# Reordering the first loads, the second half's updates at phase borders, and the panels of one output projection

## The chip, the cores and the metric

The kernel runs on one core of a Trainium2 chip. The metric is the device time of one execution in microseconds (us). Three timed runs of the kernel before gave 2873.45, 2872.70 and 2874.04 us, a median of 2873.45 us. The change is judged against these.

## The reference

A residual stream h of 256 tokens by 2048 channels (fp32) goes through two layers of mixer and SwiGLU, and then through a second block:

```
for layer in range(2):
    u = rms_norm(h, mix_norm_pre[layer])
    if layer == 0: u = even_mixer(u, ...)   # stick-breaking attention (8 heads) + gated delta rule (8 heads)
    else:          u = odd_mixer(u, ...)    # block attention (8 heads) + dilated attention (8 heads)
    h = h + rms_norm(u, mix_norm_post[layer])
    u = swiglu(rms_norm(h, ffn_norm_pre[layer]), w_gate, w_up, w_down)
    h = h + rms_norm(u, ffn_norm_post[layer])
hn = rmsnorm(h, norm_gain); proj = hn @ w_in      # second block: pool mixer + state-space mixer
h = h + concat([ya, yb]) @ w_out
h = h + (p @ w_ple) * sigmoid(h @ w_ple_gate)
return rmsnorm(h, final_gain)
```

In the even mixer, `proj = u @ w_in` gives q, k and v of the attention heads and q, k, v and z of the delta heads; the heads' outputs side by side go through `mixed @ w_out`, the output projection. Nearly all of the arithmetic is in the dense products with fp32 weights.

## The kernel before

**Products.** The 256 tokens are two tiles of 128, t = 0 and t = 1. h lies in SBUF as [128, 2, 2048]. A dense product takes the contraction dimension in steps k of 128 channels (16 for 2048 channels) and the output columns in panels of 512. One k of one panel is a *unit*. Weights and activations are each split in a high part in fp32r and a rest, so a unit is three matmuls for each t (lines 313, 314, 315):

```
PE.matmul(o, a, wh, start=u["first"], stop=False)
PE.matmul(o, a, wl, start=False, stop=False)
PE.matmul(o, b, wh, start=False, stop=u["last"])
```

where a and b are the high part and the rest of the transposed activations (uh, ul), and wh and wl those of the weights. The results of a panel gather in one of four PSUM banks (`mm`); four more (`aux`) are for everything else.

**Weights.** SP loads them in chunks of two units, 512 KB (line 212, tile `wr`, five buffers). Each is then split: ScalarE (ACT) makes wh, with the gain of the norm as scale (line 347) or without (line 228), and VectorE (DVE) makes wl (line 348 or 229). `split(upto, most)` makes splits up to a look-ahead of three to six chunks, at most `most` of them at one step.

**Order.** The program is emitted by hand: each engine runs its instructions in the order in which the code issues them. `order()` (lines 238 to 275) lists the steps of all phases. A phase is a stretch of units behind one norm. Its first 12 units (`HEAD`) are done for t = 0 alone and then for t = 1 alone, the middle ones for both, and the last 8 (`TAIL`) again for t = 0 and then for t = 1. So, at a *border* between two phases, the norm of t = 0 can be worked off while the tail of t = 1 runs. Three kinds of *hooks* are tied to step numbers: T(t, c) transposes 512 channels of h on TensorE (line 364), which ACT and DVE then split to uh and ul (lines 344 and 345); U(t, c) adds a panel to the residual on DVE (line 425); C(t) makes the factor of the post norm. Four borders matter here: the two behind the mixers of the layers, and the two behind their FFNs. In the first phase there is no such border, and hooks there load x and make the first transposes.

**Tasks.** The work of the heads (attention, delta rule) runs in generators. After each unit `tick()` lets up to three of them take one step, each after the number of ticks that its last `yield` names. A generator can also wait for a flag, such as "v" in `T["ready"]`, which is set when the last unit of that panel has been issued. `drain(sel)` steps *all* tasks, over and over, until the ones in `sel` are done. In the even mixer, this happens eleven units into the output projection (line 1022), since its units from k = 12 on read the last heads' outputs.

**Start.** Line 137 loads the identity matrix for the transposes on ACT's queue; `run_units()` (line 277) starts x, the first weights and the gains' vector (`load_gains`, line 149; tile `gsrc`). The other gains are loaded by a task in the first phase, by SP, and transposed on TensorE at line 157.

Of the kernel before, what the change touches and what calls it, by code (L numbers as in the profile page):

```python
# [10 lines left out]
F32 = mybir.dt.float32  # L11
# [9 lines left out]
P = 128  # L21
# [76 lines left out]
def trunk(ctx: ExitStack, tc: tile.TileContext, I, out):  # L98
    nc = tc.nc
# [27 lines left out]
    def ct(name):  # L127
        a, b = _COLS[name]
        return cst[:, a:b]
# [4 lines left out]

    h = cp.tile([P, 2, D], F32, name="h")
    ident = cp.tile([P, P], F32, name="ident")
    nc.scalar.dma_start(ident, ct("ident"))

    def load_x(t, c, eng=nc.sync):
        eng.dma_start(h[:, t, c * 512:(c + 1) * 512], I["x"][0, t * P:(t + 1) * P, c * 512:(c + 1) * 512])  # L140
# [17 lines left out]
        ACT.activation(gT[:, first * KT:first * KT + n], ps[:, :n], AF.Copy)  # L158

    units, chunks, tasks, now = [], [], [], [0]  # L160
    phs = []

    def phase(norm=True, begin=None):
        phs.append(dict(a=len(units), norm=norm, begin=begin))

    def gemm(src, wap, kts, panels, evac, kc=2, gi=None):

        for j, (c0, c1) in enumerate(panels):
            n = c1 - c0
            for g in range(0, len(kts), kc):  # L170
                ks = kts[g:g + kc]
                chunks.append((wap, ks, c0, c1, gi))
                for i, k in enumerate(ks):
                    units.append(dict(chunk=len(chunks) - 1, i=i, k=k, src=src, n=n, j=j, ps={},
                                      first=g + i == 0, last=g + i == len(kts) - 1, evac=evac,
                                      before=[], after=[]))
                    units[-1]["pn"] = units[-1 - g - i]["ps"]

    def spawn(gen, gap=3, delay=1):
        tasks.append(Task(gen, gap, now[0] + delay))  # L180
# [1 line left out]

    def tick():
        now[0] += 1
        left = CAP
        for tk in list(tasks):
            if left and tk.next <= now[0] and tk.step(now[0]):
                left -= 1
                tasks.remove(tk)
                tasks.append(tk)  # L190
        tasks[:] = [tk for tk in tasks if not tk.done]

    def drain(sel):
# [44 lines left out]
    def order():  # L238

        seq = []  # L240
        ends = [p["a"] for p in phs[1:]] + [len(units)]
        for pi, (p, end) in enumerate(zip(phs, ends)):
            us = units[p["a"]:end]
            nx = phs[pi + 1] if pi + 1 < len(phs) else None
            nm = p["nm"] = p.get("nm") or Norm(p)
            head, mid, tail = us[:HEAD], us[HEAD:-TAIL], us[-TAIL:]
            T = lambda t, c, n=nm: (lambda: n.T(t, c))
            U = lambda t, c: (lambda: st["upd"](t, c))
            C = lambda t: (lambda: st["post"](t))
            hooks = {1: [T(0, 1)], 2: [C(1), U(0, 3)], 4: [T(0, 2)], 6: [U(1, 0), U(1, 1)],  # L250
                     HEAD - 2: [T(1, 0)], HEAD - 1: [T(1, 1)], HEAD - 4: [U(1, 2), U(1, 3)],
                     HEAD + 2: [T(1, 2)], HEAD + 4: [T(0, 3)], HEAD + 6: [T(1, 3)], HEAD + 5: [nm.stats],
                     HEAD + 10: []}
            if pi == 0:
                X = lambda c: (lambda: [load_x(t, c) for t in range(2)])
                hooks = {0: [nm.begin, T(0, 0), T(1, 0), X(2)], 2: [T(0, 1), X(3)], 3: [T(1, 1)],
                         6: [T(0, 2)], 7: [T(1, 2)], 9: [nm.stats], 10: [T(0, 3)], 11: [T(1, 3)],
                         HEAD + 3: [lambda: spawn(load_gains(1, len(gains)))]}
            if p["begin"]:
                hooks[HEAD + (10 if pi else 3)].append(p["begin"])  # L260
            if nm.norm:
                us[KT - 1]["before"].append(lambda n=nm: drain([n.task]))
            for i, (u, t) in enumerate([(u, 0) for u in head] + [(u, 1) for u in head]):
                if pi:
                    seq.append((u, (t,), hooks.get(i, []), EXTRA if t == 0 else 0, int(i > 1)))
            seq += [(u, (0, 1), hooks.get(i, []) if pi == 0 else [], 0, 99)
                    for i, u in enumerate(mid if pi else head + mid)]
            hooks = {}
            if nx:
                n2 = nx["nm"] = Norm(nx)  # L270
                hooks = {TAIL: [C(0)], TAIL + 3: [U(0, 0), U(0, 1)], TAIL + 5: [U(0, 2)],
                         2 * TAIL - 1: [n2.begin, lambda n2=n2: n2.T(0, 0)]}
            for i, (u, t) in enumerate([(u, 0) for u in tail] + [(u, 1) for u in tail]):
                seq.append((u, (t,), hooks.get(i, []), EXTRA if nx else 0, int(not nx or t == 0 or i == TAIL + 1)))
        return seq

    def run_units():
        load_x(0, 0)
        fetch(0)
        load_x(1, 0, nc.scalar)  # L280
        g0 = load_gains(0, 1)
        next(g0)
        fetch(1)
        for t in range(2):
            load_x(t, 1)
        fetch(3)
        logexp()
        for _ in g0:
            pass
        for u, ts, hooks, lead[0], most[0] in order():  # L290
            for f in hooks:
                f()
            if 0 in ts:
                for f in u["before"]:
                    f()
            fetch(max(u["chunk"] + LA, ns[0] + LA - 1))
            while (u["chunk"], u["i"]) not in W:
                split(ns[0])
            wh, wl, si = W[u["chunk"], u["i"]]
            if 1 in ts:  # L300
                del W[u["chunk"], u["i"]]
                live[si][0] -= 1
                if not live[si][0]:
                    del live[si]
            split(si + SA + lead[0], most[0])
            n = u["n"]
            xh, xl = u["src"](u["k"])
            for t in ts:
                if u["first"]:
                    u["ps"][t] = psm.tile([P, 512], F32, name="mm", tag="mm")  # L310
                o = u["pn"][t][:, :n]
                a, b = xh[:, t * P:(t + 1) * P], xl[:, t * P:(t + 1) * P]
                PE.matmul(o, a, wh, start=u["first"], stop=False)  # L313
                PE.matmul(o, a, wl, start=False, stop=False)  # L314
                PE.matmul(o, b, wh, start=False, stop=u["last"])  # L315
            if u["last"]:
                for t in ts:
                    u["evac"](u["j"], t, u["pn"][t][:, :n])
            if 1 in ts:
                for f in u["after"]:  # L320
                    f()
            tick()
# [197 lines left out]
    def mix1():  # L520
# [16 lines left out]
        def attn_head(g, T, mask, i, qT, kT):  # L537
# [22 lines left out]
            yield  # L560
            if "v" not in T["ready"]:
                yield lambda: "v" in T["ready"]
                yield 2
            mh, ml = st["m"]
            v = T["v"].rearrange("p t (h d) -> p t h d", h=4)
            po = aux()
# [11 lines left out]
        for g in range(4):  # L578
            T = dict(ready=set())
            base = (g // 2) * 3072 + (g % 2) * 512  # L580

            def start(g=g, T=T):
                for n in "qkv":
                    T[n] = t4("tm" + n).rearrange("p (t c) -> p t c", t=2)
                done.append(spawn(attn_group(g, T)))

            for i, n in enumerate("qkv"):
                b = len(units)
                gemm(u_src, win, KTS, [(base + 1024 * i, base + 1024 * i + 512)],
                     head_evac(lambda n=n, T=T: T[n], "rq" if n == "q" else "rs", "v"), gi=2)  # L590
                units[-1]["after"].append(lambda n=n, T=T: T["ready"].add(n))
                if i == 0:
                    units[b]["before"].append(start)
        c = len(units)
# [4 lines left out]
    def mix0():  # L599
# [97 lines left out]
        def gdn(g, T):  # L697
# [16 lines left out]
            ss = sp.tile([P, 4, 4], F32, name="gss", tag="gss", bufs=2)  # L714
            for ni, n in enumerate("qkv"):
                yield lambda: n in T["ready"]
                yield 2
                y = t4("c" + n).rearrange("p (h s) -> p h s", h=4)
                for hh in range(2):
                    ps = aux()  # L720
# [221 lines left out]
        def sb_head(g, T, i, qT, kT):  # L942
# [21 lines left out]
            T["s"] = True  # L964
            yield 1
            ACT.activation(zm, zm, AF.Exp)
            yield
            if "v" not in T["ready"]:
                yield lambda: "v" in T["ready"]
                yield 2  # L970
            mh, ml = st["mh"][0]
            v = T["v"].rearrange("p t (h d) -> p t h d", h=4)
            po = aux()
# [21 lines left out]
        for g in range(2):  # L995
            for kind, T, base in (("g", GT[g], 3072 + 512 * g), ("s", ST[g], 512 * g)):
                for i, n in enumerate("qkv"):
# [9 lines left out]
                    units[-1]["after"].append(lambda n=n, T=T: T["ready"].add(n))  # L1007
# [9 lines left out]
            gemm(u_src, win, KTS, [(6144 + 512 * g, 6656 + 512 * g)], z_evac(GT[g]), gi=0)  # L1017
            units[-1]["after"].append(lambda T=GT[g]: T["ready"].add("z"))
        c = len(units)
        gemm(h_src, I["ev_w_out"][0], KTS, cols(4), post_evac)  # L1020
        units[c]["before"] += [post_begin, lambda: load_post(I["mix_norm_post"][0])]
        units[c + 11]["before"].append(lambda: drain(list(done)))

    ssm = {}

# [585 lines left out]
```

## Time and profile before

| | |
|---|---|
| median of 3 runs | 2873.45 us |
| time of the profiled execution | 2871.88 us |
| span of its trace | 2870.1 us |
| mean granted TensorE clock | 0.994 of full speed |
| TensorE (PE) busy | 2819.5 us, 98% |
| VectorE (DVE) busy | 1771.5 us, 62% |
| ScalarE (ACT) busy | 1503.6 us, 52% |
| GpSimd (POOL) busy | 192.2 us, 7% |

The page of the profile gives each engine's busy time, with the matmuls and the loads of their weights (PEld) apart. Then come views of single stretches: a timeline lists instructions with start and length, and in brackets how long the engine stood idle before them and whom it waited for; a view of the waits sums that by what was waited for; a view of windows gives for a stretch the busy time of each engine and the clock that TensorE was granted (1.00 is 2.4 GHz, 0.50 is 1.2 GHz). The busy share of 98% is TensorE's, and it is an average: the 2% are not spread evenly.

### The profile page before, as it was taken

What the parts mean: (1) busy time and instruction counts of PE and PEld (TensorE: products, weight loads), DVE (VectorE), ACT (ScalarE), POOL (GpSimd) and SP (SyncE); (2) the same over time, 40 slices, a digit from 0 to 9 for tenths busy, and PEclk for the clock granted to TensorE, in tenths of its full rate; (3) what the DMA queues carried; (4) which work ended last, traced back from release to release, by engine and by line L of the source; (5) the groups of instructions that cost most, each with busy time, mean ns of one, the idle gap of its engine ahead of it and who ended that gap; (6) DMA issues with size and microseconds to landing.
All of it is one profiled execution on the core that took longest, in us unless ns stands there. A gap on an engine that the chain in (4) does not pass through costs nothing.

```text
span 2870.1 us, 36735 instructions
## 1 busy us (share of the span) xinstructions
PE 2819.5 (98%) x13503; PEld 2314.3 (81%) x13503; DVE 1771.5 (62%) x2701; ACT 1503.6 (52%) x2374; POOL 192.2 (7%) x290
## 2 busy tenths in 40 slices
PE   7999999999999999999999999999999999999998
PEld 5878877788888878878888878888888887878887
DVE  4776755678666666566666565545555556565555
ACT  4656554655555445446555465445544545555444
POOL 0140510000000011010000000000000001100000
PEclk9999999999999999999999999999999999999999
DMA  6564655576677767755556556666666665875654
GB/s 202 169 172 147 181 155 169 173 195 197 221 211 210 218 211 215 252 185 162 173 172 187 185 171 190 186 196 189 187 194 194 191 203 169 296 268 168 193 190 149
DMA packets 303621, 552.23 MB, mean 192 GB/s; under 512 B 43032, under 2 KB 48720, under 8 KB 303440
## 3 DMA queue, kind: packets, MB, share of 16 engines
q1 hardware_dynamic: 292896, 515.20, 58.9%
q0 software_dynamic: 10224, 34.35, 3.7%
q8 instruction: 106, 1.74, 0.2%
q14 instruction: 75, 0.61, 0.1%
q10 hardware_dynamic: 320, 0.34, 0.0%
HBM read 532.24 MB, written 21.76 MB: 193 GB/s over the span
## 4 chain that ended last, share of the span: by engine, by line
PE 94%; DVE 2%; ACT 1%; DMA 1%; issue 1%; SPq 0%; POOL 0%; ACTq 0%; POOLq 0%; DVEq 0%
PE mm L313 29%; PE mm L315 29%; PE mm L314 29%; PE aux L451 1%; DVE wl L348 1%; ACT wh L347 1%; PE aux L364 1%; PE aux L1344 0%; DMA wr<-in_ffn_w_up_dram 0%; DMA b<-in_b_im_dram 0%; DMA mb<-xs 0%; PE aux L1434 0%; PE aux L1203 0%; PE aux L540 0%; PE aux L567 0%
## 5 line engine op out<-in xcount | busy, mean ns | idle before, releaser
L348 DVE SCALAR_TENSOR_TENSOR wl<-wr,gT,wh 128x512 fp32r<-128x512 f32 x1248 | 881.8, 750 | 555.3 <-ACT wh L347 554.1
L347 ACT ACTIVATE wh<-wr,gT 128x512 fp32r<-128x512 f32 x1248 | 828.9, 716 | 529.9 <-PE mm L315 497.5
L313 PE MATMUL mm<-wh,uh 128*128 128x512 f32 x2624 | 1054.8, 402 | 1.3 <-ACT wh L347 1.3
L315 PE MATMUL mm<-wh,ul 128*128 128x512 f32 x2624 | 1028.1, 392 | 1.4 <-DVE ul L345 1.4
L314 PE MATMUL mm<-wl,uh 128*128 128x512 f32 x2624 | 1026.2, 391 | 0.2 <-DVE wl L348 0.2
L229 DVE TENSOR_TENSOR wl<-wr,wh 128x1024 fp32r<-128x1024 f32 x324 | 401.1, 1242 | 360.0 <-ACT wh L228 359.5
L315 PEld LDWEIGHTS mm<-wh,ul 128*128 128x128 f32 x2624 | 494.4, 188 | 110.9 <-DVE ul L345 5.3
L313 PEld LDWEIGHTS mm<-wh,uh 128*128 128x128 f32 x2624 | 495.3, 189 | 104.7 <-issue 5.7
L314 PEld LDWEIGHTS mm<-wl,uh 128*128 128x128 f32 x2624 | 495.5, 189 | 97.3 <-DVE wl L348 1.8
L228 ACT ACTIVATE wh<-wr 128x1024 fp32r<-128x1024 f32 x324 | 342.4, 1059 | 402.0 <-PE mm L315 397.2
L313 PE MATMUL mm<-wh,mh 128*128 128x512 f32 x832 | 326.5, 392 | 0.0
L315 PE MATMUL mm<-wh,ml 128*128 128x512 f32 x832 | 324.0, 389 | 0.0
L314 PE MATMUL mm<-wl,mh 128*128 128x512 f32 x832 | 323.8, 389 | 0.0
L313 PEld LDWEIGHTS mm<-wh,mh 128*128 128x128 f32 x832 | 156.2, 188 | 32.9 <-issue 1.4
L315 PEld LDWEIGHTS mm<-wh,ml 128*128 128x128 f32 x832 | 156.2, 188 | 32.7
L314 PEld LDWEIGHTS mm<-wl,mh 128*128 128x128 f32 x832 | 156.3, 188 | 31.5
L489 POOL TENSOR_TENSOR acc<-acc,wpost 128x512 f32<-128x512 f32 x12 | 15.3, 1300 | 789.7 <-ACT junk L335 789.7
L345 DVE TENSOR_TENSOR ul<-aux,uh 128x512 fp32r<-128x512 f32 x48 | 33.1, 689 | 56.0 <-ACT uh L344 55.8
L344 ACT ACTIVATE uh<-aux 128x512 fp32r<-128x512 f32 x48 | 28.5, 594 | 74.7 <-PE aux L364 74.7
L344 ACT ACTIVATE mh<-aux 128x512 fp32r<-128x512 f32 (+1 forms) x60 | 32.6, 543 | 52.5 <-PE aux L451 39.6
L345 DVE TENSOR_TENSOR ml<-aux,mh 128x512 fp32r<-128x512 f32 (+1 forms) x60 | 37.2, 619 | 36.3 <-ACT mh L344 35.3
L364 PE MATMUL aux<-ident,h 128*128 128x128 f32 x192 | 32.6, 299 | 8.8 <-DVE h L425 8.8
(445 smaller groups left out, 2014.1 us busy)
## 6 DMA issues: line engine op xcount, KB each, us to landing
wr<-in_ffn_w_gate_dram SPq DMA_DIRECT2D x176, 512.0 KB, 4.1
wr<-in_ffn_w_up_dram SPq DMA_DIRECT2D x176, 512.0 KB, 4.1
wr<-in_ffn_w_down_dram SPq DMA_DIRECT2D x176, 512.0 KB, 4.6
wr<-in_ev_w_in_dram SPq DMA_DIRECT2D x112, 512.0 KB, 3.8
wr<-in_od_w_in_dram SPq DMA_DIRECT2D x96, 512.0 KB, 3.7
wr<-in_w_in_dram SPq DMA_DIRECT2D x64, 512.0 KB, 4.9
wr<-in_ev_w_out_dram SPq DMA_DIRECT2D x32, 512.0 KB, 4.4
wr<-in_od_w_out_dram SPq DMA_DIRECT2D x32, 512.0 KB, 4.5
```

What stands on the lines that cost most here:

```text
L228: ACT.activation(hi, r[:, k:k + m, :], AF.Copy)
L229: DVE.tensor_sub(lo, r[:, k:k + m, :], hi.bitcast(F32))
L313: PE.matmul(o, a, wh, start=u["first"], stop=False)
L314: PE.matmul(o, a, wl, start=False, stop=False)
L315: PE.matmul(o, b, wh, start=False, stop=u["last"])
L344: ACT.activation(hi, src, AF.Copy)
L345: DVE.tensor_sub(lo, src, hi.bitcast(F32))
L347: ACT.activation(hi, src, AF.Copy, scale=gain)
L348: DVE.scalar_tensor_tensor(lo, src, gain, hi.bitcast(F32), OP.mult, OP.subtract)
L364: PE.transpose(p4[:, i * P:(i + 1) * P], h[:, t, k * P:(k + 1) * P], ident)
L451: PE.transpose(p4[:, i * P:(i + 1) * P], src[:, i * P:(i + 1) * P], ident)
L489: POOL.tensor_mul(acc, acc, cut(st["wpost"], j))
```

## The change

The changed kernel (a) loads the identity on SP's queue, and on ACT's queue the first gains ahead of x; (b) in the first phase does the first two units for t = 0 alone and then for t = 1, with the transposes T(1, 0) between them; (c) at borders moves U(1, 0) and U(1, 1) from step 6 to step 4 and U(1, 3) from step 8 to step 12, and makes at most one weight split at step 2 and at each step from 5 on (before: at each from 2 on), and one at the last tail step in place of one at the tail's second step for t = 1; (d) in the even mixer's output projection does k = 0 to 11 of panels 0 and 1 and then k = 12 to 15 of both, drains three tasks one after the other at units 0, 4 and 8, and all of them at unit 24; (e) sets the flags of q, k and v three ticks later, and drops the pause of two ticks that a task made after such a wait (some pauses stay), and one task waits 4 ticks instead of 2 behind an Exp. The weight vectors named in the diff's `load_gains` are loaded by the same lines as before.

```diff
-    nc.scalar.dma_start(ident, ct("ident"))
+    nc.sync.dma_start(ident, ct("ident"))
...
+        steps = [(j, 0, len(kts)) for j in range(len(panels))]
+        if late:
+            steps[:2] = [(0, 0, late), (1, 0, late), (0, late, len(kts)), (1, late, len(kts))]
...
     def tick():
         now[0] += 1
+        for d in [d for d in due if d[0] <= now[0]]:
+            due.remove(d)
+            d[1]()
...
+    def later(n, f):
+        due.append((now[0] + n, f))
...
     def drain(sel):
         while any(not x.done for x in sel):
+            for d in due:
+                d[1]()
+            due.clear()
...
-            hooks = {1: [T(0, 1)], 2: [C(1), U(0, 3)], 4: [T(0, 2)], 6: [U(1, 0), U(1, 1)],
-                     HEAD - 2: [T(1, 0)], HEAD - 1: [T(1, 1)], HEAD - 4: [U(1, 2), U(1, 3)],
-                     HEAD + 2: [T(1, 2)], HEAD + 4: [T(0, 3)], HEAD + 6: [T(1, 3)], HEAD + 5: [nm.stats],
+            hooks = {1: [T(0, 1)], 2: [C(1), U(0, 3)], 4: [T(0, 2), U(1, 0), U(1, 1)],
+                     HEAD - 2: [T(1, 0)], HEAD - 1: [T(1, 1)], HEAD - 4: [U(1, 2)],
+                     HEAD: [U(1, 3)], HEAD + 2: [T(1, 2)], HEAD + 4: [T(0, 3)], HEAD + 6: [T(1, 3)], HEAD + 5: [nm.stats],
...
-                hooks = {0: [nm.begin, T(0, 0), T(1, 0), X(2)], 2: [T(0, 1), X(3)], 3: [T(1, 1)],
+                hooks = {(0, 0): [nm.begin, T(0, 0), X(2)], (1, 0): [T(1, 0)], 2: [T(0, 1), X(3)], 3: [T(1, 1)],
...
-                    seq.append((u, (t,), hooks.get(i, []), EXTRA if t == 0 else 0, int(i > 1)))
+                    seq.append((u, (t,), hooks.get(i, []), EXTRA if t == 0 else 0, int(i == 2 or i > 4)))
+            if pi == 0:
+                seq += [(u, (t,), hooks.get((t, i), []), 0, 99) for t in range(2) for i, u in enumerate(head[:2])]
...
-                         2 * TAIL - 1: [n2.begin, lambda n2=n2: n2.T(0, 0)]}
+                         2 * TAIL - 1: [n2.begin, lambda n2=n2: n2.T(0, 0), lambda: split(len(parts), 1)]}
...
-                seq.append((u, (t,), hooks.get(i, []), EXTRA if nx else 0, int(not nx or t == 0 or i == TAIL + 1)))
+                seq.append((u, (t,), hooks.get(i, []), EXTRA if nx else 0, int(not nx or t == 0)))
...
     def run_units():
-        load_x(0, 0)
-        fetch(0)
-        load_x(1, 0, nc.scalar)
         g0 = load_gains(0, 1)
         next(g0)
+        load_x(0, 0)
+        load_x(1, 0, nc.scalar)
         fetch(1)
...
             for ni, n in enumerate("qkv"):
                 yield lambda: n in T["ready"]
-                yield 2
...
             ACT.activation(zm, zm, AF.Exp)
-            yield
+            yield 4
             if "v" not in T["ready"]:
                 yield lambda: "v" in T["ready"]
-                yield 2
...
-                    units[-1]["after"].append(lambda n=n, T=T: T["ready"].add(n))
+                    units[-1]["after"].append(lambda n=n, T=T: later(3, lambda: T["ready"].add(n)))
...
-        gemm(h_src, I["ev_w_out"][0], KTS, cols(4), post_evac)
+        gemm(h_src, I["ev_w_out"][0], KTS, cols(4), post_evac, late=12)
         units[c]["before"] += [post_begin, lambda: load_post(I["mix_norm_post"][0])]
-        units[c + 11]["before"].append(lambda: drain(list(done)))
+        for i, x in ((0, 2), (4, 4), (8, 1)):
+            units[c + i]["before"].append(lambda x=x: drain(done[x:x + 1]))
+        units[c + 24]["before"].append(lambda: drain(list(done)))
```

Three places show how instructions move. The first is ScalarE's program at its start, before: loads on its queue, the gains' copy (gT), the splits of x (uh) and of the weights (wh).

```order
L137 DMA ident<-in_cst_dram 128x128
L140 DMA h<-in_x_dram 128x512
L153 DMA gsrc<-in_mix_norm_pre_dram 16x128
L133 ACT_TABLE_LOAD
L158 ACTIVATE gT<-aux 128x16
L344 ACTIVATE uh<-aux 128x4x128 x2
L347 ACTIVATE wh<-wr,gT 128x512 x8
```

And after (the lines are numbered some 13 higher there):

```order
L153 DMA gsrc<-in_mix_norm_pre_dram 16x128
L140 DMA h<-in_x_dram 128x512
L133 ACT_TABLE_LOAD
L158 ACTIVATE gT<-aux 128x16
L358 ACTIVATE uh<-aux 128x4x128
L361 ACTIVATE wh<-wr,gT 128x512 x8
L358 ACTIVATE uh<-aux 128x4x128 x2
```

The second half's uh now stands behind eight wh. The second place is VectorE's program at the border from the first FFN to the odd mixer, before: residual updates (h), rests of the activations (ul) and of the weights (wl), the last tail result (acc) and the post norm's factor (ms).

```order
L425 SCALAR_TENSOR_TENSOR h<-acc,rp,h 128x512 x3
L345 TENSOR_TENSOR ul<-aux,uh 128x4x128
L485 TENSOR_TENSOR acc<-mm,acc 128x512
L345 TENSOR_TENSOR ul<-aux,uh 128x4x128
L329 TENSOR_REDUCE ms<-ssp 128x1
L330 TENSOR_SCALAR ms<-ms 128x1
L421 TENSOR_TENSOR acc<-acc,wpost 128x512
L425 SCALAR_TENSOR_TENSOR h<-acc,rp,h 128x512
L348 SCALAR_TENSOR_TENSOR wl<-wr,gT,wh 128x512 x4
L345 TENSOR_TENSOR ul<-aux,uh 128x4x128
L348 SCALAR_TENSOR_TENSOR wl<-wr,gT,wh 128x512 x4
L425 SCALAR_TENSOR_TENSOR h<-acc,rp,h 128x512 x4
```

And after, from the rest of the first transposes on:

```order
L359 TENSOR_TENSOR ul<-aux,uh 128x4x128
L362 SCALAR_TENSOR_TENSOR wl<-wr,gT,wh 128x512 x2
L499 TENSOR_TENSOR acc<-mm,acc 128x512
L359 TENSOR_TENSOR ul<-aux,uh 128x4x128
L343 TENSOR_REDUCE ms<-ssp 128x1
L344 TENSOR_SCALAR ms<-ms 128x1
L435 TENSOR_TENSOR acc<-acc,wpost 128x512
L439 SCALAR_TENSOR_TENSOR h<-acc,rp,h 128x512
L362 SCALAR_TENSOR_TENSOR wl<-wr,gT,wh 128x512 x2
L359 TENSOR_TENSOR ul<-aux,uh 128x4x128
L439 SCALAR_TENSOR_TENSOR h<-acc,rp,h 128x512 x2
L362 SCALAR_TENSOR_TENSOR wl<-wr,gT,wh 128x512 x4
```

Behind these stand one more h, two ul, the last h and three ul. The four updates of the second half, one piece before, now stand in three pieces, the first two ahead of four wl. The third place is VectorE's program where the last delta heads end in the even mixer's output projection, before: gf and gw are factors of the heads' norm, o the heads' outputs, mg their split parts.

```order
L843 TENSOR_REDUCE gf<-osq 128x4
L844 TENSOR_TENSOR gw<-grs 128x8
L845 TENSOR_TENSOR gf<-gf,gw 128x8
L846 TENSOR_SCALAR gf<-gf 128x8
L849 TENSOR_TENSOR gf<-gw,grs 128x8
L856 SCALAR_TENSOR_TENSOR o_3876<-o_3876,gf,tmz 128x128 x4
L856 SCALAR_TENSOR_TENSOR o_3910<-o_3910,gf,tmz 128x128 x4
L345 TENSOR_TENSOR mg<-aux,mg 128x4x128 x2
L229 TENSOR_TENSOR wl<-wr,wh 128x1024 x2
```

And after:

```order
L855 TENSOR_REDUCE gf<-osq 128x4
L856 TENSOR_TENSOR gw<-grs 128x8
L857 TENSOR_TENSOR gf<-gf,gw 128x8
L858 TENSOR_SCALAR gf<-gf 128x8
L242 TENSOR_TENSOR wl<-wr,wh 128x1024 x2
L861 TENSOR_TENSOR gf<-gw,grs 128x8
L242 TENSOR_TENSOR wl<-wr,wh 128x1024
L868 SCALAR_TENSOR_TENSOR o_3871<-o_3871,gf,tmz 128x128 x4
L868 SCALAR_TENSOR_TENSOR o_3910<-o_3910,gf,tmz 128x128 x4
L242 TENSOR_TENSOR wl<-wr,wh 128x1024 x2
L359 TENSOR_TENSOR mg<-aux,mg 128x4x128
L242 TENSOR_TENSOR wl<-wr,wh 128x1024
```

Before, the chain to mg has no weight split in it; after, five weight splits, two units each, stand between its members.

## Rows read from the trace of the kernel before

**Rows 1.** The page's head: span, and busy time of each engine.

```profile
span 2870.1 us, 36735 instructions
...
PE 2819.5 (98%) x13503; PEld 2314.3 (81%) x13503; DVE 1771.5 (62%) x2701; ACT 1503.6 (52%) x2374; POOL 192.2 (7%) x290
```

**Rows 2.** Waits of PE: what for, us in total, times, longest.

```profile
PE aux L157 <- DMA gsrc<-in_norm_gain_dram: 9.7, 1, 9.7
PE aux L364 <- DVE h L425: 8.8, 4, 2.2
PE aux L157 <- DMA gsrc<-in_mix_norm_pre_dram: 7.3, 1, 7.3
PE aux L451 <- DVE o L856: 4.5, 1, 4.5
PE aux L974 <- DVE tmv L1004: 2.6, 1, 2.6
PE aux L974 <- ACT zm L966: 1.6, 1, 1.6
```

**Rows 3.** Windows: length, busy us by engine (instructions), clock, DMA share, GB/s.

```profile
47.50:51.30 3.80, 3.73 (x10) 3.00 (x11) 1.64 (x4) 1.33 (x4) 0.00 (x0) 0.50 0.96 226
...
438.50:443.90 5.40, 5.18 (x16) 3.94 (x17) 3.39 (x10) 1.46 (x3) 0.00 (x0) 0.50 0.00 2
...
1283.61:1287.00 3.39, 2.82 (x11) 2.46 (x12) 3.01 (x5) 0.60 (x1) 0.00 (x0) 0.50 0.87 314
```

**Rows 4.** Timeline of the border behind the first FFN: start, us, engine, line.

```profile
1273.25 0.68 DVE L485 TENSOR_TENSOR acc<-mm,acc 128x512 f32<-128x512 f32 x1
...
1274.65 0.58 ACT L344 ACTIVATE uh<-aux 128x512 fp32r<-128x512 f32 x1
...
1277.39 2.73 DVE L348 SCALAR_TENSOR_TENSOR wl<-wr,gT,wh 128x512 fp32r<-128x512 f32 x4
...
1280.04 0.68 DVE L345 TENSOR_TENSOR ul<-aux,uh 128x512 fp32r<-128x512 f32 x1
...
1280.78 0.50 PE L315 MATMUL mm<-wh,ul 128*128 128x512 f32 x1 [0.69 <-DVE ul L345]
...
1281.11 0.40 PE L313 MATMUL mm<-wh,uh 128*128 128x512 f32 x1
...
1281.57 0.40 PE L315 MATMUL mm<-wh,ul 128*128 128x512 f32 x1
1283.29 2.73 DVE L425 SCALAR_TENSOR_TENSOR h<-acc,rp,h 128x512 f32<-128x512 f32 x4
...
1284.18 1.08 PE L364 MATMUL aux<-ident,h 128*128 128x128 f32 x4 [2.21 <-DVE h L425]
...
1289.21 0.60 PE L364 MATMUL aux<-ident,h 128*128 128x128 f32 x4
```

**Rows 5.** Timeline of the border behind the first mixer.

```profile
524.74 2.74 DVE L425 SCALAR_TENSOR_TENSOR h<-acc,rp,h 128x512 f32<-128x512 f32 x4
...
530.93 0.60 PE L364 MATMUL aux<-ident,h 128*128 128x128 f32 x4
```

**Rows 6.** Timeline of ACT in the even mixer.

```profile
364.30 2.02 ACT L886 ACTIVATE X<-mb 128x1024 f32<-128x1024 f32 x1 [7.28 <-DMA mb<-xs]
```

**Rows 7.** Timeline of the start.

```profile
9.99 5.00 ACT L347 ACTIVATE wh<-wr,gT 128x512 fp32r<-128x512 f32 x8
...
10.76 0.80 PE L313 MATMUL mm<-wh,uh 128*128 128x512 f32 x1 [1.30 <-ACT wh L347]
...
16.40 0.42 PE L364 MATMUL aux<-ident,h 128*128 128x128 f32 x1
```

**Rows 8.** DMA issues from 4.9 to 5.3 and 6.5 to 6.7 us: KB, us to landing.

```profile
wr<-in_ev_w_in_dram SPq DMA_DIRECT2D x1, 512.0 KB, 5.9
...
h<-in_x_dram SPq DMA_DIRECT2D x1, 256.0 KB, 6.3
```

**Rows 9.** Waits of SP from 33 to 41 us.

```profile
SPq L612 <- DVE cs L611: 6.2, 1, 6.2
```

More of the change, by code (lines that the diff above doesn't have):

```diff
@@ L160, in trunk, with gemm @@
     units, chunks, tasks, now = [], [], [], [0]
-    phs = []
+    phs, due = [], []
     def phase(norm=True, begin=None):
         phs.append(dict(a=len(units), norm=norm, begin=begin))
-    def gemm(src, wap, kts, panels, evac, kc=2, gi=None):
-        for j, (c0, c1) in enumerate(panels):
+    def gemm(src, wap, kts, panels, evac, kc=2, gi=None, late=None):
+        steps = [(j, 0, len(kts)) for j in range(len(panels))]
+        if late:
+            steps[:2] = [(0, 0, late), (1, 0, late), (0, late, len(kts)), (1, late, len(kts))]
+        pss = [{} for _ in panels]
+        for j, g0, g1 in steps:
+            c0, c1 = panels[j]
             n = c1 - c0
-            for g in range(0, len(kts), kc):
+            for g in range(g0, g1, kc):
                 ks = kts[g:g + kc]
@@ L173, in gemm @@
                 for i, k in enumerate(ks):
-                    units.append(dict(chunk=len(chunks) - 1, i=i, k=k, src=src, n=n, j=j, ps={},
+                    units.append(dict(chunk=len(chunks) - 1, i=i, k=k, src=src, n=n, j=j, pn=pss[j],
                                       first=g + i == 0, last=g + i == len(kts) - 1, evac=evac,
                                       before=[], after=[]))
-                    units[-1]["pn"] = units[-1 - g - i]["ps"]
     def spawn(gen, gap=3, delay=1):
@@ L264, in order @@
                 if pi:
-                    seq.append((u, (t,), hooks.get(i, []), EXTRA if t == 0 else 0, int(i > 1)))
+                    seq.append((u, (t,), hooks.get(i, []), EXTRA if t == 0 else 0, int(i == 2 or i > 4)))
+            if pi == 0:
+                seq += [(u, (t,), hooks.get((t, i), []), 0, 99) for t in range(2) for i, u in enumerate(head[:2])]
             seq += [(u, (0, 1), hooks.get(i, []) if pi == 0 else [], 0, 99)
-                    for i, u in enumerate(mid if pi else head + mid)]
+                    for i, u in enumerate(mid if pi else head + mid) if pi or i > 1]
             hooks = {}
@@ L309, in run_units @@
                 if u["first"]:
-                    u["ps"][t] = psm.tile([P, 512], F32, name="mm", tag="mm")
+                    u["pn"][t] = psm.tile([P, 512], F32, name="mm", tag="mm")
                 o = u["pn"][t][:, :n]
@@ L966, in sb_head @@
             ACT.activation(zm, zm, AF.Exp)
-            yield
+            yield 4
             if "v" not in T["ready"]:
                 yield lambda: "v" in T["ready"]
-                yield 2
             mh, ml = st["mh"][0]
@@ L1006, in mix0 @@
                     gemm(u_src, win, KTS, [(base + 1024 * i, base + 1024 * i + 512)], ev, gi=0)
-                    units[-1]["after"].append(lambda n=n, T=T: T["ready"].add(n))
+                    units[-1]["after"].append(lambda n=n, T=T: later(3, lambda: T["ready"].add(n)))
                     if i == 0:
```

## Prediction

> **What bounds the kernel now.** I read the page's head first: TensorE works 2819.5 of 2870.1 us [rows 1], so in most stretches nothing but its own matmuls sets the time, and an edit can only give back what lies in the other 50.6 us, or in stretches where it works at half clock. The second view is PE's waits [rows 2]. Six kinds make up most of the idle time: 9.7 and 7.3 us for the gains' vectors, 8.8 us in four pieces of up to 2.2 for the residual update h at phase borders, 4.5 us for the delta heads' outputs o, 2.6 us for an evacuated v (tmv), and 1.6 us for an Exp (zm). The third is the windows behind the waits [rows 3]: after three of these kinds of wait TensorE runs 3.4 to 5.4 us at a granted clock of 0.50, which is 1.2 GHz, though it has work. So a wait costs itself and about half of the stretch behind it. Then I read the timelines of these places to see who is late and why [rows 4 to 9].
>
> **Borders (part c).** At the border behind the first FFN, DVE makes four wl of 0.68 us each in one piece, twice, before it comes to the four updates of the second half at 1283.29; T(1, 0) waits 2.21 us for the first of them, and starts at 1284.18 [rows 4]. Before that, a product waits 0.69 us for ul. The window from 1283.61 on is 3.39 us at 0.50, which costs 1.7 [rows 3]. In all 2.21 + 0.69 + 1.7 = 4.6 us.
>
> The changed order on DVE, laid out with the durations of [rows 4] (0.68 for each of wl, ul, acc and an update): after the first ul two wl go first, from 1273.3 to 1274.65, so acc comes 1.4 us later than at 1273.25, and so does the square sum on ACT behind it and uh of T(0, 1), 1276.0 for 1274.65. Its ul ends at about 1277.3: TensorE's fifth unit waits 0.3. The factor, U(0, 3) and two wl follow to 1280.1; the ul of T(0, 2) ends at 1280.75, as before. Now come U(1, 0), U(1, 1), to 1282.1, four wl to 1284.75, U(1, 2), and the ul of T(1, 0), which ends at 1286.05. TensorE has T(1, 0)'s input at 1281.5 and starts it at 1281.75 without a wait; its eleventh unit waits 0.5 for the last wl needed; the first unit for t = 1 then waits 1.3 for that ul. With a matmul each 0.23 us (1281.11 to 1281.57 holds two steps [rows 4]), T(1, 2) comes at 1287.0 instead of 1289.21: 2.2 us gained. The same table for the border behind the second FFN gives 2.4. Behind a mixer there is no late acc, and U starts at 524.74 [rows 5]; laid out in the same way only a wait of 0.65 for ul stays, and T(1, 2) comes at 527.2 instead of 530.93: 3.7, twice. Sum: 2.2 + 2.4 + 7.4 = −12.0; I take −11.8, since the second mixer's row is a little shorter. What I choose here is that waits of at most 1.3 us leave the clock up. The row for it is the 0.69 us wait at 1280.78, behind which matmuls still follow at 0.23 [rows 4]; 2.21 us is followed by half clock. Between them no row tells, at full clock. The bounds: 0 if the waits and the clock stay as they are, and −18 if no wait is left (4.2 to 4.8 at each border).
>
> The Trainium skill, "TensorE: Matmul & The Clock Gate", section "What's actually happening", says that "the default state is throttled, and activity releases the throttle". By that, a wait shorter than the one removed could still bring the half clock; the rows agree that it follows waits of 2.2 us and more, and no row shows 1.3. By it the borders would give less, which is the second rival.
>
> **Output projection (part d).** Before, the drain eleven units in steps all tasks until the delta heads are done, so the chain gf, gw, o, mg is issued in one go with no unit between; TensorE waits 4.5 us for o [rows 2] and then runs 5.40 us at 0.50, 2.7 lost [rows 3]. After, all drains find their tasks done or near it, since thirteen units of 3 × 2 × 0.23 = 1.38 us, 17.9 us, are added ahead of the last one, and five weight splits stand between the members of the chain. What is next late is the last transposes of o, about one unit ahead of their use: at most 1.0 us is left. Four PSUM banks are held by panels 0 and 1; panel 2 starts four units (5.5 us) after panel 0 ends, which covers its evacuation. Term: −7.2 (range −7.2 to −6.2 with that, and +2 if the banks were late).
>
> **Even mixer (part e).** The 2.6 us wait for tmv is a product issued right behind the unit that ends v. With the flag three ticks later it comes at least two units, 2.8 us, behind: −2.6. The 1.6 us wait for zm goes too (4 ticks instead of 1 behind the Exp), but ACT stands 7.28 us for X at 364.30 [rows 6] and other small work of the heads is now queued behind it: I count 0 for the pair. Reordered tasks meet new places; no row shows how late each is. The nearest rows are the mixer's two waits of 1.6 and 2.6 us [rows 2]; I put +1.5, with −3 (the 1.6 and some others go) and +8 (three waits like 2.6) as ends.
>
> **Start (parts a, b).** The gains' vector heads ACT's queue and lands earlier, so the first product no longer waits for the second half's uh: about 7.9 instead of 10.76 [rows 7]. But only four unit halves follow; the rest needs uh of T(1, 0), which on ACT now stands behind eight wh of 0.63 us (5.00 for eight [rows 7]), and the last two of these need the fourth weight chunk. That chunk lands between those of 4.96 + 5.9 = 10.9 and 6.58 + 6.3 = 12.9 [rows 8], about 12.1. wh ends at 13.4, uh at 14.05, ul at 14.85, and T(0, 1) starts at 16.6 instead of 16.40: +0.2. So TensorE starts earlier and waits in the middle. Ends: −2.8 if the chunk comes early, +1.9 if the stretch after the new wait runs as the 3.80 us at 0.50 behind the 9.7 us wait did [rows 3], half of which is lost.
>
> **What stays.** The 9.7 us wait for norm_gain and its 1.9 of half clock: SP stands 6.2 us for a memset of DVE (cs) ahead of those loads [rows 9], and behind T(0, 1) all queues read as before. The splits made at other steps are hidden by DVE's 38% and ACT's 48% of idle time [rows 1], except at the borders, where they are in the table above.
>
> **Sum.** −11.8 − 7.2 − 2.6 + 1.5 + 0.2 = −19.9. The profiled execution took 2871.88 us (its span of 2870.1 and 1.8 around it), so 2852.0; the median of the runs is 1.57 higher, which gives **2853.5 us**. No change means within 0.2%, 5.7 us, about what a measurement can tell.
>
> **Rivals.**
> 1. *The wait moves to ul of T(1, 0).* At all four borders the wait of 1.3 comes out near the 2.2 that it replaces, and the clock still falls. For it: U(1, 2) and four wl stand ahead of that ul. Against: two updates are out of the way. Borders then give about −1: total −9, 2864. Chance 0.16.
> 2. *Short waits keep the half clock.* At each border the 1.7 stays, and 1.9 comes at the start: −19.9 + 6.8 + 1.9 = −11.2, 2862. For it: [rows 3] show it after each long wait; against: 1280.78 [rows 4]. Chance 0.10.
> 3. *No wait is left at all.* Borders −18, start −2.8, mixer −3, instead of my values: −19.9 − 6.2 − 3.0 − 4.5 = −33.6, 2840. For it: DVE has slack if ACT's square sum comes sooner than laid out. Chance 0.08.
> 4. *Slower: the dropped pauses make heads' products meet their evacuations.* Place: the eight attention heads' products with v and six convolution steps of the delta heads; each would wait as tmv does now, 2.62 us, 14 × 2.62 = 36.7. Without my +1.5 the rest is −21.4, so it decides from more than eight of the fourteen on; all would give +15.3, 2889. For it: the pause behind the wait is gone in both. Against: the flag is set three ticks later, which is as long as the pause and the tick it replaces. Chance 0.06.
>
> **Chances and range.** My forecast, with sizes off by a few us, 0.60. The range leaves the fourth rival out, and half of the third: 2844 to 2866. Faster by over 0.2% 0.87 (the forecast, the second and third, most of the first), same 0.07, slower 0.06.
>
> **What would show it.** Right: the line of waits for h gone or under 1 us, the wait for o gone, in the windows behind them a clock of 1.00, the wait for tmv gone, a new wait of TensorE around 10 to 14 us for uh of t = 1, and the wait of 9.7 unchanged. Wrong: windows at 0.50 behind waits for ul at the borders (rivals 1 and 2), or many new waits for tmq, tmk or tmv in the first 430 us (rival 4).

## The result, and the profile after

The changed kernel takes 2848.68 us (median of 4 runs, 2848.36 to 2849.59), the kernel before beside it 2873.74 (2872.70 to 2874.45): a ratio of 0.9914, with a 95% interval of 0.9896 to 0.9931. It is 25.1 us faster; 19.9 were forecast, and 2848.68 lies in the range of 2844 to 2866. The profiled executions took 2871.88 us before, 1.9 below that median, and 2849.59 after, 0.9 above its own, so the spans differ by only 22.3 us. The head of the page, after:

```profile
span 2847.8 us, 36740 instructions
...
PE 2811.0 (99%) x13503; PEld 2308.0 (81%) x13503; DVE 1771.2 (62%) x2701; ACT 1503.7 (53%) x2374; POOL 192.5 (7%) x290
```

Against [rows 1], TensorE has the same 13503 matmuls in 8.5 us less of busy time, which fits the half clock that went. The other 13.8 us of the span are idle time. PE's waits after:

```profile
PE aux L157 <- DMA gsrc<-in_norm_gain_dram: 10.6, 1, 10.6
PE mm L329 <- DVE ul L359: 3.5, 7, 0.9
PE aux L157 <- DMA ident<-in_cst_dram: 3.0, 1, 3.0
PE aux L378 <- DMA h<-in_x_dram: 2.9, 1, 2.9
PE mm L327 <- ACT uh L358: 2.4, 1, 2.4
PE mm L327 <- ACT wh L361: 1.3, 1, 1.3
PE aux L1357 <- DVE zs L1422: 0.7, 1, 0.7
```

Of the six lines of [rows 2] four are gone: h at the borders, o, tmv and zm. The 7.3 us for the first gains have become 3.0 for the identity and 2.9 for x, and the 9.7 us for norm_gain are 10.6. In place of h there are waits for ul, none over 0.9 us. The timeline of the border behind the first FFN, to be held against [rows 4] (the whole lies 16.1 us earlier now):

```profile
1263.98 0.68 DVE L359 TENSOR_TENSOR ul<-aux,uh 128x512 fp32r<-128x512 f32 x1
...
1264.59 1.41 DVE L439 SCALAR_TENSOR_TENSOR h<-acc,rp,h 128x512 f32<-128x512 f32 x2
...
1265.75 0.60 PE L378 MATMUL aux<-ident,h 128*128 128x128 f32 x4
...
1265.91 2.74 DVE L362 SCALAR_TENSOR_TENSOR wl<-wr,gT,wh 128x512 fp32r<-128x512 f32 x4
...
1269.22 1.28 DVE L359 TENSOR_TENSOR ul<-aux,uh 128x512 fp32r<-128x512 f32 x2
...
1269.96 0.50 PE L329 MATMUL mm<-wh,ul 128*128 128x512 f32 x1 [0.92 <-DVE ul L359]
...
1271.00 0.60 PE L378 MATMUL aux<-ident,h 128*128 128x128 f32 x4
```

The two updates now stand ahead of the four wl, and T(1, 0), at 1265.75, waits for nothing. The row at 1269.96 is the new wait, 0.92 us for the ul of T(1, 0). The border's first transpose is at 1271.35 before and at 1255.28 here; T(1, 2), at 1289.21 before and in the last row here, so comes 2.1 us sooner within the border. The waits there, 2.9 us before, are 1.3 now (0.40 and 0.92). The windows behind the places of [rows 3], after:

```profile
15.88:19.00 3.12, 3.12 (x9) 2.57 (x10) 0.00 (x0) 0.16 (x1) 0.00 (x0) 0.50 1.05 388
...
50.10:53.50 3.40, 3.40 (x9) 2.71 (x10) 1.90 (x4) 1.03 (x3) 0.00 (x0) 0.54 0.93 290
417.00:427.00 10.00, 10.00 (x54) 8.54 (x53) 4.69 (x7) 3.18 (x3) 1.04 (x1) 1.00 0.50 156
...
1268.00:1272.00 4.00, 3.08 (x16) 2.24 (x15) 3.17 (x5) 0.89 (x2) 0.00 (x0) 1.00 0.74 221
```

At the output projection (417 to 427) TensorE is busy throughout at full clock, and at the border the clock is full too. The start after:

```profile
8.54 0.80 PE L327 MATMUL mm<-wh,uh 128*128 128x512 f32 x1 [1.30 <-ACT wh L361]
...
11.69 2.70 ACT L361 ACTIVATE wh<-wr,gT 128x512 fp32r<-128x512 f32 x4 [1.36 <-DMA wr<-in_ev_w_in_dram]
...
14.29 0.57 ACT L358 ACTIVATE uh<-aux 128x512 fp32r<-128x512 f32 x1
14.92 0.50 PE L327 MATMUL mm<-wh,uh 128*128 128x512 f32 x1 [2.36 <-ACT uh L358]
...
17.75 1.05 PE L378 MATMUL aux<-ident,h 128*128 128x128 f32 x4
```

The first product comes 2.2 us earlier than in [rows 7], but the one at 14.92 waits 2.36 us for uh, which stands behind eight wh on ACT, and T(0, 1) is at 17.75 instead of 16.40.

The 0.50 from 15.88 on looks new, but the pace is not. In the kernel before, products stand 0.42 to 0.43 us apart from 12.14 up to T(0, 1), and 0.23 apart only from 17.50 on. Four products of before, two on either side of T(0, 1), and behind them its window view:

```profile
15.55 0.63 PE L314 MATMUL mm<-wl,uh 128*128 128x512 f32 x1
...
15.98 0.63 PE L315 MATMUL mm<-wh,ul 128*128 128x512 f32 x1
...
17.73 0.40 PE L315 MATMUL mm<-wh,ul 128*128 128x512 f32 x1
...
17.96 0.39 PE L313 MATMUL mm<-wh,uh 128*128 128x512 f32 x1
```

```profile
10.76:16.40 5.64, 5.64 (x12) 4.02 (x13) 5.37 (x9) 4.23 (x7) 0.00 (x0) 1.00 1.03 370
```

Two products of the changed kernel, inside the window at 0.50:

```profile
16.47 0.63 PE L327 MATMUL mm<-wh,uh 128*128 128x512 f32 x1
...
16.90 0.63 PE L328 MATMUL mm<-wl,uh 128*128 128x512 f32 x1
```

The steps are the same, 0.43 us, though one window says 1.00 and the other 0.50. So at the very start of a trace the steps of the products have to be read, and not that column.

From the starts of the same transposes in both traces, the time from the first transpose of abw (64.77 before, 66.96 after) on splits so, in us: the even mixer and its output projection to T(0, 0) of the first border 448.94, now 434.35 (−14.6); the four borders, first to last transpose of each, −3.6, −2.2, −3.5, −2.4 (−11.7 together); what lies before abw +2.2, of which 1.6 are there at T(1, 3) (33.00 for 31.38) and the rest comes with the longer wait for norm_gain; the rest of the trace, above all the second block, +1.8.

### The profile page after: what moved, and what is told of

Its sections match the earlier page's. It is cut to its first block, busy times and chain, and to the rows that moved or that the text cites. A ratio compares the mean times of both kernels' runs of the same rounds, so it can differ in the third digit from the quotient of the medians.

```text
span 2847.8 us, 36740 instructions
## 1 busy us (share of the span) xinstructions
PE 2811.0 (99%) x13503; PEld 2308.0 (81%) x13503; DVE 1771.2 (62%) x2701; ACT 1503.7 (53%) x2374; POOL 192.5 (7%) x290
## 4 chain that ended last, share of the span: by engine, by line
PE 94%; DVE 3%; DMA 2%; ACT 1%; issue 1%; SPq 1%; ACTq 0%; POOLq 0%; POOL 0%; DVEq 0%
PE mm L327 29%; PE mm L329 29%; PE mm L328 29%; DVE wl L362 1%; PE aux L465 1%; DMA wr<-in_w_in_dram 1%; PE aux L378 0%; ACT wh L361 0%; DVE h L439 0%; DVE ul L359 0%; PE aux L1357 0%; DMA wr<-in_ffn_w_up_dram 0%; DMA wr<-in_ev_w_in_dram 0%; DMA b<-in_b_im_dram 0%; PE aux L1447 0%
## 5 line engine op out<-in xcount | busy, mean ns | idle before, releaser
L328 PEld LDWEIGHTS mm<-wl,mh 128*128 128x128 f32 x832 | 156.3, 188 | 31.4
L358 ACT ACTIVATE mh<-aux 128x512 fp32r<-128x512 f32 (+1 forms) x60 | 32.4, 540 | 55.8 <-PE aux L465 39.6
L345 POOL TENSOR_TENSOR rp<-ms,half 128x1 f32<-128x1 f32 x8 | 6.7, 837 | 471.8 <-DVE ms L344 471.8
```

Of the source, the lines that this page charges most:

```text
L345: POOL.tensor_tensor(r[:, t:t + 1], m, half[:, 0:1], OP.pow)
L358: ACT.activation(hi, src, AF.Copy)
```

## The experiments

The first four do one part each on the kernel before. Their expectations were written with the two traces above at hand.

**Part (c) alone.**

```diff
-  4: [T(0, 2)], 6: [U(1, 0), U(1, 1)], HEAD - 4: [U(1, 2), U(1, 3)]
+  4: [T(0, 2), U(1, 0), U(1, 1)], HEAD - 4: [U(1, 2)], HEAD: [U(1, 3)]
...
-  int(i > 1)
+  int(i == 2 or i > 4)
```

> The kernel before with part (c) alone: the updates U(1, c) and the weight splits at borders. Theory: at each border the wait for h of 2.2 us goes, waits for ul of 0.4 to 1.1 us take its place, and the clock stays at 1.00; the four borders give 11.6 us, so about 2862, and start, mixer and output projection stay as they were (9.7, 2.6, 1.6 and 4.5 us of waits). Rival: the border gain needs the other parts (the tasks of part e stand on the same engines), and less than 8 us comes.

Measured: 2862.34 us, before 2873.43; ratio 0.9963 (0.9950 to 0.9977), 11.1 us. The wait for h is gone, and the waits for o, tmv and zm are as before; that for norm_gain is 10.8 for 9.7, and those for ul are 3.3 in six pieces for 1.4 in two. The interval alone (6.6 to 14.4 us) does not shut out the rival's 8, but the trace does: its four borders are 11.7 us shorter, as in the changed kernel. The theory holds.

**Part (d) alone.**

```diff
-  gemm(h_src, I["ev_w_out"][0], KTS, cols(4), post_evac)
+  gemm(h_src, I["ev_w_out"][0], KTS, cols(4), post_evac, late=12)
...
-  units[c + 11]["before"].append(lambda: drain(list(done)))
+  for i, x in ((0, 2), (4, 4), (8, 1)):
+      units[c + i]["before"].append(lambda x=x: drain(done[x:x + 1]))
+  units[c + 24]["before"].append(lambda: drain(list(done)))
```

(and `gemm` with the argument `late`, as in the change.)

> The kernel before with part (d) alone: panels 0 and 1 of the even mixer's output projection in two pieces, and the drains later. Theory: the wait of 4.5 us for o and 5.4 us at half clock go, 7.2 us, so about 2866.5. Rival: without the changed flags the last attention heads are still open at the earlier drains, which then step all tasks in one go and wait there, so that less than 4 us comes.

Measured: 2866.08 us; ratio 0.9975 (0.9966 to 0.9983), 7.4 us. No wait of PE shows from 420 to 450 us, and it works there without a gap at full clock:

```profile
427.00:433.00 6.00, 6.00 (x32) 5.10 (x31) 2.76 (x4) 2.12 (x2) 1.04 (x1) 1.00 0.59 173
433.00:440.00 7.00, 7.00 (x33) 5.79 (x32) 4.45 (x8) 2.88 (x3) 1.66 (x1) 1.00 0.47 154
```

The drains need nothing of part (e). The two edits of this part, the split panels and the later drains, were not run apart.

**Part (e) alone.**

```diff
-  units[-1]["after"].append(lambda n=n, T=T: T["ready"].add(n))
+  units[-1]["after"].append(lambda n=n, T=T: later(3, lambda: T["ready"].add(n)))
...
   ACT.activation(zm, zm, AF.Exp)
-  yield
+  yield 4
```

(and the pauses behind the waits dropped, as in the change.)

> The kernel before with part (e) alone: flags of q, k, v three ticks later, pauses dropped, 4 ticks behind the Exp. Theory: the waits for tmv (2.6 us), zm (1.6) and X (1.5) and some small ones in the mixer go, 7.4 us, so about 2866.3, with no change at the borders. Rival (the prediction's count): 1.1 us, as new waits take the place of some; then the other 6 us of the mixer came with the split of the output projection or by the shift in time that the start brings.

Measured: 2865.92 us; ratio 0.9973 (0.9963 to 0.9983), 7.5 us. From 80 to 500 us one wait of PE is left, the one that part (d) removes:

```profile
PE aux L460 <- DVE o L863: 4.5, 1, 4.5
```

The waits for tmv, zm and X are all gone, and no new one is there. The load of mb, from which X is made, is issued at 343.64 us here and at 356.96 before, and ACT no longer stands for it. The rival, the prediction's count of 1.1 us, is wrong. Which of the three edits of this part removes which wait was not run apart.

**Parts (a) and (b) alone.**

```diff
-  nc.scalar.dma_start(ident, ct("ident"))
+  nc.sync.dma_start(ident, ct("ident"))
...
-  hooks = {0: [nm.begin, T(0, 0), T(1, 0), X(2)], ...
+  hooks = {(0, 0): [nm.begin, T(0, 0), X(2)], (1, 0): [T(1, 0)], ...
...
```

(and the order of the loads in `run_units` and the steps of the first two units, as in the change.)

> The kernel before with parts (a) and (b) alone: loads of the start and first steps. Theory: the first product comes 2.2 us earlier, but TensorE then waits 2.4 us for uh of the second half and runs three us at half clock, so everything from 20 us on is 2.2 us later: about 2876. Rival (the prediction): +0.2, 2874; the rest of the 2.2 would be scatter between executions.

Measured: 2875.17 us; ratio 1.0007 (0.9998 to 1.0016). The interval takes in no change, so this run alone does not decide between the two. The four parts add up to −11.1 − 7.4 − 7.5 + 1.7 = −24.3, against −25.1 for all together.

The next ones start from the changed kernel. **Without (a) and (b).**

```diff
-  nc.sync.dma_start(ident, ct("ident"))
+  nc.scalar.dma_start(ident, ct("ident"))
...
-  hooks = {(0, 0): [nm.begin, T(0, 0), X(2)], (1, 0): [T(1, 0)], ...
+  hooks = {0: [nm.begin, T(0, 0), T(1, 0), X(2)], ...
...
```

(and the other lines of the two parts.)

> The changed kernel with parts (a) and (b) undone. Theory: the parts are additive, so it is faster than the changed kernel by what these two cost alone, 1.7 to 2.2 us: about 2846.7. Rival: the early stretch and the rest interact, and it comes out level with the changed kernel, 2848.7.

Measured: 2846.10 us (2845.72 to 2847.31); ratio to before 0.9905 (0.9890 to 0.9920). Its slowest run, 2847.31, is below the fastest of the changed kernel, 2848.36; the medians are 2.6 us apart. So the start costs time, as its traces show.

**Without (b) alone.**

```diff
-  hooks = {(0, 0): [nm.begin, T(0, 0), X(2)], (1, 0): [T(1, 0)], ...
+  hooks = {0: [nm.begin, T(0, 0), T(1, 0), X(2)], ...
...
```

(and the steps of the first two units as before.)

> The changed kernel with part (b) undone: the loads in the new order, but T(1, 0) ahead of the first product as before, so that uh of the second half stands before the weights' splits on ACT. Theory: the loss at the start is the order of uh behind eight wh, so the wait of 2.4 us and the half clock behind it go, and the first product comes at about 9.3 instead of 10.76: 3 us less than the changed kernel, about 2845.5. Rival: the fourth weight chunk (landing near 12) sets the pace in any case, and nothing is gained against the changed kernel.

Measured: 2845.27 us; ratio to before 0.9902 (0.9889 to 0.9916), 3.4 us less than the changed kernel.

```profile
9.23 0.79 PE L325 MATMUL mm<-wh,uh 128*128 128x512 f32 x1 [1.29 <-ACT wh L359]
...
14.00 0.60 PE L376 MATMUL aux<-ident,h 128*128 128x128 f32 x4
```

The first product is later than in the changed kernel (9.23 for 8.54), T(0, 1) is earlier (14.00 for 17.75), and no product in between waits for uh. So by the medians (b) costs 3.4 us and (a) gives 0.8, the latter within the scatter of the runs. The traces order the three starts without overlap: T(1, 3), the last transposes of this stretch, start at 29.8 to 31.4 us in the five kernels with the old start (before, at 31.38, is the latest of them), at 32.4 to 33.9 in the six with the new one, and at 28.55 here and 29.08 in the last run below, with the new loads and the old order.

**The other gains' loads first.**

```diff
+  def early():
+      g = load_gains(1, len(gains))
+      next(g)
+      spawn(g, delay=13)
...
-  HEAD + 3: [lambda: spawn(load_gains(1, len(gains)))]}
+  HEAD + 3: [early]}
```

> The changed kernel with one edit more: SP issues the five loads of the other gains ahead of the even mixer's constants instead of behind them; their transpose on TensorE stays where it is. Theory: the wait of 10.6 us is SP standing 6 us for DVE's memset of cs ahead of these loads; issued near 35 us they land near 40, so the wait falls under 1.5 us and the half clock behind it (about 1.9) goes: 11 us less, about 2837.5. Rival: another load behind them is late next (the weights that follow, or abw for the small projection), and less than 5 us comes.

Measured: 2842.69 us; ratio to before 0.9893 (0.9880 to 0.9907), 6.0 less than the changed kernel. The wait of 10.6 is gone, since the gains land before TensorE comes to their transpose. The rival's other load is there, but the gain is half of the theory's 11 rather than below 5:

```profile
PE aux L671 <- ACT abs L363: 4.5, 1, 4.5
```

```profile
49.60:52.40 2.80, 2.80 (x15) 1.89 (x15) 2.80 (x5) 1.89 (x4) 0.00 (x0) 0.52 0.65 249
```

The first row is of PE's waits, the second a window behind the wait: 4.5 us for abs, which is made from abw, and half clock.

**The old splits.**

```diff
-  int(i == 2 or i > 4)
+  int(i > 1)
...
-  2 * TAIL - 1: [n2.begin, lambda n2=n2: n2.T(0, 0), lambda: split(len(parts), 1)]}
+  2 * TAIL - 1: [n2.begin, lambda n2=n2: n2.T(0, 0)]}
```

(and the tail's second step for t = 1 makes a split again.)

> The changed kernel with the updates U where the change puts them, but the weight splits at borders as before (one at every step from 2 on, and one at the tail's second step for t = 1). Theory: the wait for h is removed by the place of U(1, 0) and U(1, 1) alone, ahead of four wl; the splits' places decide only which ul is late, so the borders keep about 10 of their 11.6 us: 2850. Rival: with a split at steps 3 and 4 four wl stay ahead of U(1, 0), the wait for h stays above 1.5 us and the clock falls: 2856 or more.

Measured: 2851.75 us; ratio to before 0.9925 (0.9912 to 0.9937). No wait for h is left; from first to last transpose the borders give 2.4, 2.2, 2.4 and 2.4 us. That is 9.4 of 11.7: the theory's 10, nearly. The splits' new places are worth 2.3 in the traces (3.1 by the medians), all of it behind the mixers.

**The old places of the updates, with the new splits.**

```diff
-  4: [T(0, 2), U(1, 0), U(1, 1)], HEAD - 4: [U(1, 2)], HEAD: [U(1, 3)]
+  4: [T(0, 2)], 6: [U(1, 0), U(1, 1)], HEAD - 4: [U(1, 2), U(1, 3)]
```

> The changed kernel with the updates U at their old steps (6 and 8), and the weight splits at borders where the change puts them. Theory: what decides is how many wl stand between the ul of T(0, 2) and the update U(1, 0); here two instead of four, so the wait for h falls from 2.2 to about 0.8 us, the clock stays at 1.00, and the borders keep some 9 of 11.6 us: 2851. Rival: the place of the updates alone removes the wait; here it stays near 2.2 with half clock behind it, and the time is 2858 or more.

Measured: 2851.89 us; ratio to before 0.9923 (0.9910 to 0.9937). Two rows of the timeline of the border behind the first FFN:

```profile
1265.42 1.40 DVE L362 SCALAR_TENSOR_TENSOR wl<-wr,gT,wh 128x512 fp32r<-128x512 f32 x2
...
1267.63 0.63 PE L378 MATMUL aux<-ident,h 128*128 128x128 f32 x4 [0.88 <-DVE h L439]
```

Two wl instead of four ahead of the update leave 0.88 of the 2.21 us, and the clock is not lost; the borders keep 9.0 us. Either half of part (c) does most of it by itself, because both shorten the same queue on DVE.

**Gains and abw first.**

```diff
+  st["abw"] = t2("abw", S).rearrange("p (k n) -> p k n", n=16)
+  nc.sync.dma_start(st["abw"], I["ev_w_in"][0][:, 7168:7184].rearrange("(k p) n -> p k n", p=P))
...
-  r = t2("abw", S).rearrange("p (k n) -> p k n", n=16)
-  nc.sync.dma_start(r, win[:, 7168:7184].rearrange("(k p) n -> p k n", p=P))
+  r = st["abw"]
```

(the new load stands in `early`, behind `next(g)`.)

> The changed kernel with the five loads of the gains and the load of abw (the small projection's weights) ahead of the even mixer's constants. Theory: with the gains alone ahead, 4.5 us of wait for abs and 1.9 us of half clock stayed, because abw was issued behind the same memset of cs and landed at 48; ahead of it, it lands near 42 and both go: about 2837. Rival: DVE's product with the gains stands behind ACT's copy gT and the memsets and is late by itself, or the next weight chunks now come later; then 2 us at most come, 2841.

Measured: 2840.44 us; ratio to before 0.9883 (0.9869 to 0.9896), 2.3 less than with the gains alone; at the first transposes of the first border it is 2.7 ahead (491.95 for 494.63). The rival's number is nearer: 1.8 us for abs stay. Two rows of the timeline ahead of it:

```profile
46.75 0.17 DVE L407 TENSOR_SCALAR rq<-rs 128x2 f32<-128x2 f32 x1 [2.94 <-POOL rs L405]
46.83 0.42 DVE L664 TENSOR_TENSOR abw<-abw,gT 128x256 f32<-128x256 f32 x1
```

DVE stands 2.94 us for the norm's factor from POOL, and the product with abw is queued behind that. The load is no longer what it waits for, and neither are the copy gT and the memsets that the rival named.

**The same, and (b) undone.**

```diff
-  hooks = {(0, 0): [nm.begin, T(0, 0), X(2)], (1, 0): [T(1, 0)], ...
+  hooks = {0: [nm.begin, T(0, 0), T(1, 0), X(2)], ...
```

> The kernel of the run before with part (b) undone as well, so that T(1, 0) stands ahead of the first product. Theory: the gains add up, 3.4 us for (b) undone and 11.5 for the loads: about 2834. Rival: the 3.4 us were partly time at which TensorE now waits for weights, since 385 to 390 GB/s are moved in the first 18 us in each of these kernels; then about 2836.

Measured: 2835.82 us (2834.06 to 2836.59); ratio to before 0.9867 (0.9854 to 0.9881). It is 12.9 us faster than the changed kernel, and the fastest of all here. The rival's 2836 is what came, but not for its reason: undoing (b) gave 4.6 us here, more than the theory's 3.4, and what is short are the loads, 8.2 for 11.5. In the traces T(1, 3) is 4.8 us ahead of the run before (29.08 for 33.85), and the first border 3.1 (488.85 for 491.95). The difference is half clock behind the wait for abs, which the run before does not have, with the same wait:

```profile
44.55:47.50 2.95, 2.95 (x15) 2.02 (x14) 2.80 (x5) 0.83 (x2) 0.00 (x0) 0.50 1.02 394
```

```profile
49.00:53.00 4.00, 4.00 (x38) 3.31 (x36) 3.12 (x5) 1.15 (x2) 0.00 (x0) 1.00 1.03 389
```

The first is of this kernel, behind a wait of 1.78 us, the second of the one before, behind 1.77. Why the clock fell in one of them only is not shown.

## Why the prediction was right, and where it was off

*Borders.* Right in mechanism and size: −11.8 forecast, −11.1 measured alone, −11.7 in the trace. The waits for ul came out at 0.9 us, under the 1.3 laid out, and the clock stayed up. That it would was a choice without a row; it is now shown for waits of up to 0.92 us here, and not for 1.3. Rivals 1 and 2 fall at the borders. Rival 3 falls there too (−11.1 for its −18) and at the start; only the mixer went its way, and beyond its −3.

*Output projection.* Right: −7.2 forecast, −7.4 measured alone. No wait is left there, so the four banks, two for each panel, were not late.

*Even mixer.* The term was mis-sized: −2.6 + 1.5 = −1.1 forecast, −7.5 measured, outside its own ends (−5.6 at the lower one). The step "I count 0 for the pair" fails: the wait for zm went, and X's went as well (1.5 us of PE, which the forecast had not priced), while the "+1.5" for new waits had nothing behind it in the run. What else went, some 1.8 us, is not accounted for. Part of it may be half clock behind tmv, which some executions have and others not (last section). The forecast also put the pause behind the Exp at one tick before; the heads' tasks step every two ticks, so it was 4 instead of 2, as the list of changes says. Rival 4 is refuted by the run of part (e): none of the fourteen products waits. Its counter-argument, that the flag's three ticks replace the pause, fits this; dropped pauses without the later flags were not run.

*Start.* The step "+0.2" was too low: 1.7 alone, 2.6 by undoing it, 1.6 in the trace at T(1, 3). The step that failed is "wh ends at 13.4". It let only the last two wh wait for a chunk of weights. In the run the last four stand until 11.69 for the third chunk, and end at 14.39. So uh ends at 14.86 (forecast 14.05) and ul at 15.83 (14.85), and T(0, 1) starts at 17.75 (16.6). The half clock behind the wait of 2.36 us is not what was missed: before has the same steps up to T(0, 1), and the forecast's own 2.55 us for the six products behind uh are 0.42 each. It does last longer: steps of 0.23 begin at 17.5 us before and at 19.3 in the changed kernel. The reference was late as well: with the old start T(0, 1) is at 16.40 in before and at 15.2 to 15.8 in the four other traces.

*What stays.* The wait for norm_gain stayed, and SP's 6.2 us for cs with it. It is 0.9 longer, because the load landed 5.1 us after its issue instead of 4.2. Nothing in its chain was changed, and of the ten traces that have this wait two show 9.7 and eight 10.5 to 10.9, among them three with the old start and one part alone. So it is scatter.

*Not forecast.* The rest of the trace is 1.8 us longer after, with 0.7 and 0.4 us of waits for zs and vw in the second block. The code of the second block is the same in all runs. From the last transposes of the fourth border to the first ones behind the second block, the thirteen traces take 334.5 to 337.1 us (before 334.5, after 336.1, part (c) alone 334.5), so it is scatter between executions; what makes it is not shown.

So the total is −19.9 − 6.4 (mixer) + 1.5 (start) + 0.7 (borders) − 0.2 (output projection) = −24.3, the sum of the four single runs; the error is the mixer's term, and the start hid a part of it. The two misses have opposite signs, but the range did not need that: without the start's 1.5 us it would still hold the time. One reading of the forecast goes too far: the half clock does not follow every wait "of 2.2 us and more", as the last section shows.

## What to carry to other kernels

Where TensorE is 98% busy, look for the few stretches where a short queue on another engine stands ahead of what it needs, and count the instructions between: here four wl of 0.68 us ahead of an update cost 2.2 us of waiting and mostly 1.7 of half clock at each border, and moving either the updates or the splits removes most of it. Starting the first product earlier gains nothing if the operand of the second half is then issued behind eight others on the same engine. When a wait is removed, read which load stands behind the same obstacle: behind the gains stood abw; moving the gains' loads alone gave 6.0 us, and both together 8.2.

## What the runs showed of the hardware that was not expected

In these traces the length of a wait does not decide whether the clock falls. The wait of 2.62 us for tmv is followed by full clock in before (first row below) and by half clock in the trace of part (c) alone (second row), though it is 2.62 us there too. And the same border wait of 2.21 us in one execution, that of part (d) alone, is followed by half clock behind the first FFN and by full clock behind the second mixer (the last two rows):

```profile
185.50:189.00 3.50, 3.50 (x16) 2.73 (x17) 3.28 (x6) 2.40 (x5) 0.00 (x0) 1.00 0.52 150
```

```profile
185.80:189.00 3.20, 2.89 (x8) 2.45 (x9) 2.48 (x6) 1.24 (x3) 0.00 (x0) 0.50 0.57 165
```

```profile
1278.00:1280.00 2.00, 2.00 (x8) 1.61 (x8) 2.00 (x4) 0.60 (x1) 0.00 (x0) 0.50 0.91 318
1669.50:1672.50 3.00, 2.27 (x14) 2.02 (x15) 3.00 (x5) 1.06 (x2) 0.00 (x0) 1.00 0.89 311
```

Four traces have the old borders, with 16 such waits of 2.2 us in all; behind 15 of them the clock falls. So the 1.7 us that the forecast added at each border come mostly, not always. What tells the cases apart is not shown here.
